# A hybrid transformer layer with 32 experts on one core: expert weights in 2 MB loads with 16 KB rows, other places for them, and side work moved from GpSimd to VectorE

## The chip, the core and the metric

The kernel runs on one core of a Trainium2 chip. TensorE (PE in the profile) multiplies, VectorE (DVE) and ScalarE (ACT) do the elementwise work, GpSimd (POOL) some more of it, and SyncE (SP) issues nearly all DMAs from one queue, in the order in which they are written. Sixteen DMA engines bring the weights from HBM into SBUF. The metric is the device time of one execution in microseconds; less is better. A difference of 0.3% is about what a measurement of this kernel can tell from no change.

## The reference, cut to what matters

One layer over 256 latent tokens that also read 256 context tokens, width 1024, all in float32:

```python
u, uc = modulate(rmsnorm(x, g1), sh1, sc1), modulate(rmsnorm(ctx, g1), sh1c, sc1c)
p = split_proj(u, w_in)               # q k v of an mLSTM, q k v of a differential attention, gates
a = mlstm(p)                          # 4 heads, both directions
b = diff_attention(p, rope)           # 8 heads, rotary embedding on the latent tokens' q and k
y = (sigmoid(p[8]) * (a @ w_a) + sigmoid(p[9]) * (b @ w_b)) @ w_o
x = x + g1 * y
x = x + g2 * moe_ffn(modulate(rmsnorm(x), sh2, sc2))   # router, top 4 of 32 experts
out = rmsnorm(x, final_g)
# an expert: h = t @ w1 + b1  (1024 -> 2048);  act = min(h1,7)*sigmoid(1.702*h1)*(clip(h2)+1);  act @ w2 + b2
```

Each expert has 8 MB of w1 and 4 MB of w2 (in units of 1048576 bytes, as all MB of loads in this document), and all 32 are read in full: 384 MB.

## The kernel before

**Two halves.** The first part (the "front", to about 500 us) does everything up to the router; the rest is a loop over 16 pairs of experts. Both are written out in one program whose order is fixed in the code for each engine.

**The front.** A list of chunks, each a product of the tokens with 512 columns of a weight, runs in steps of 128 rows (`Chunk.step`, 12 matmuls: L572 to L574 and L582 to L584). Every float32 weight is split two steps ahead (`LOOK`) into two float32r halves: ACT casts `wh` (L558), DVE subtracts to get `wl` (L559). After each step `work.tick()` advances generators that do the side work by one `yield` each: `attention` runs `mlstm_unit` (eight units, one started every five ticks: row broadcast L391, exponentials, `Dm` times scores L410, products L420) and then `diff_unit`; `rope_work` turns k and q (`dk`, `dq`) with two shuffles and one product on DVE (L670, L672) and two operations on POOL (L671, L673); `late_b` adds the two gated branches on POOL (L759), casts the sum to `yh` on ACT (L760) and subtracts on DVE (L761); then `scaled_columns` multiplies half of `w_out` by its gate row, on POOL (L829). `ada_rest` (L303) is more DVE work of this kind. `need(...)` in a chunk's `before` or `mid` runs the generators until those named are done.

**The expert loop.** For each expert `expert` adds XG @ w1 to a bias already in PSUM (`bias_of`, L801; w1 at L1044), evaluates the activation on DVE and ACT (L1049 to L1053), does work for other pairs (`between`: bias of the outputs once, scatter L1080, gather L1018, transposes), transposes the activation (L1057) and multiplies by w2 (L1066). PSUM has four `acc` banks; an expert's hidden layer takes two.

**The places.** An expert's weights come as twelve loads of 1 MB, 8 KB in each of 128 partitions: `epiece` takes load n into place `ORDER[n % 18]`. Four places are the front's weight ring (`w`, number 0 in `ORDER`), fourteen (`v1_` to `v14_`) are laid over the front's other buffers after these are closed. A load is issued when the last reader of what lay in its place is done, and SP issues in order: a load that waits holds up all loads written behind it. In the trace the tiles of places are called `v__` and a number, or `w`.

The functions that the change touches, and what calls them:

## Time and profile before

| | |
|---|---|
| median of 3 runs | 1454.1 us (1451.03 to 1454.37) |
| the profiled execution | 1450.5 us, of it the span from first to last instruction 1448.9 us |
| PE, DVE, ACT, POOL busy | 93%, 37%, 19%, 6% of the span |
| front | 0 to about 500 us |
| expert loop | 500 to about 1434 us |
| DMA in the expert loop | 421 GB/s from 550 to 1400 us |

The page cuts the span into 40 slices of 36.2 us. PE's busy share is no measure of how near it is to its peak, because matmuls overlap and their ends are modelled; what matters is which wait ends last in each stretch.

### The profile page before, as it was taken

How to read it: one execution, taken by the hardware profiler on the slowest of the kernel's cores; microseconds unless marked ns; L12 is line 12 of the kernel's file. 1: busy time of each engine (PE TensorE's matmuls, PEld its weight loads, DVE VectorE, ACT ScalarE, POOL GpSimd, SP SyncE). 2: the span in 40 equal slices, each digit the busy share in tenths (PEclk: the TensorE clock that was granted, in tenths of full speed). 3: DMA queues.
4: the chain of work that ended last, by engine and by line, in shares of the span. 5: the costliest groups of instructions: out<-in, count | busy, mean ns of one | idle time of the engine just before them, and what ended most of it. 6: DMA issues, size and time to landing. Idle time of an engine off the chain costs nothing. (4 is left out here: it accounts for less than half of the span.)

```text
span 1448.9 us, 17248 instructions
## 1 busy us (share of the span) xinstructions
PE 1342.2 (93%) x6981; PEld 713.8 (49%) x6981; DVE 538.2 (37%) x1012; ACT 274.4 (19%) x569; POOL 91.7 (6%) x89
## 2 busy tenths in 40 slices
PE   5999899999998999999999999999999999999995
PEld 4778777778997633333333433333333333333331
DVE  3586765776677622221221221221212212122113
ACT  3423335435644300000000000000000000000001
POOL 0030111120024100000000000000000000000000
PEclk9999999999999989999999999999999999999998
DMA  8575353123379599999999999999999999999993
GB/s 354 212 266 191 133 182 116 59 88 117 128 279 399 214 362 421 420 421 420 422 421 420 421 421 420 421 421 420 421 421 421 420 421 421 421 422 420 421 421 157
DMA packets 68801, 483.90 MB, mean 334 GB/s; under 512 B 8355, under 2 KB 8612, under 8 KB 10604
## 3 DMA queue, kind: packets, MB, share of 16 engines
q1 hardware_dynamic: 67948, 480.36, 81.8%
q0 software_dynamic: 768, 2.38, 0.4%
q8 instruction: 57, 0.93, 0.3%
q14 instruction: 28, 0.23, 0.0%
HBM read 481.64 MB, written 1.06 MB: 333 GB/s over the span
## 5 line engine op out<-in xcount | busy, mean ns | idle before, releaser
L1049 DVE TENSOR_SCALAR eg<-acc 128x512 f32<-128x512 f32 x32 | 22.1, 692 | 450.8 <-PE acc L1044 450.8
L1050 ACT ACTIVATE es<-eg 128x512 f32<-128x512 f32 x32 | 20.2, 630 | 742.8 <-DVE eg L1049 742.8
L1074 DVE TENSOR_TENSOR Y<-py,g2r 64x512 f32<-64x512 f32 x64 | 44.1, 689 | 276.0 <-PE py L1066 275.3
L559 DVE TENSOR_TENSOR wl<-w,wh 128x512 fp32r<-128x512 f32 (+1 forms) x160 | 111.1, 703 | 88.0 <-ACT wh L558 87.3
L1044 PE MATMUL acc<-w,XG 128*64 128x512 f32 x512 | 116.1, 595 | 4.9 <-DMA w<-in_w_dram 4.9
L582 PE MATMUL acc<-uh,wh 128*128 128x256 f32 (+1 forms) x328 | 109.1, 333 | 0.1
L584 PE MATMUL acc<-uh,wl 128*128 128x256 f32 (+1 forms) x328 | 105.0, 320 | 2.9 <-DVE wl L559 2.9
L558 ACT CAST wh<-w 128x512 fp32r<-128x512 f32 (+1 forms) x160 | 93.0, 603 | 61.9 <-PE acc L574 31.3
L583 PE MATMUL acc<-ul,wh 128*128 128x256 f32 (+1 forms) x328 | 104.6, 319 | 0.0
L1044 PEld LDWEIGHTS acc<-w,XG 128*64 128x64 f32 x512 | 35.5, 137 | 82.2 <-issue 65.1
L582 PEld LDWEIGHTS acc<-uh,wh 128*128 128x128 f32 x328 | 62.5, 191 | 12.3 <-ACT wh L558 3.4
L584 PEld LDWEIGHTS acc<-uh,wl 128*128 128x128 f32 x328 | 62.3, 190 | 8.8 <-DVE wl L559 4.1
L572 PE MATMUL acc<-wh,uh 128*128 128x512 f32 x160 | 65.0, 406 | 0.7 <-DVE gi L340 0.7
L583 PEld LDWEIGHTS acc<-ul,wh 128*128 128x128 f32 x328 | 62.4, 190 | 4.4 <-DVE ul L286 0.3
L1018 PEld LDWEIGHTS pga<-P,u 128*128 128x128 f32 x512 | 58.4, 192 | 12.5 <-DVE eg L1049 12.2
L573 PE MATMUL acc<-wl,uh 128*128 128x512 f32 x160 | 63.4, 396 | 0.2 <-DVE wl L559 0.2
L574 PE MATMUL acc<-wh,ul 128*128 128x512 f32 x160 | 63.2, 395 | 0.0
L801 PE MATMUL acc<-b1s,cst 128*64 128x512 f32 x256 | 61.7, 603 | 0.0
L1018 PE MATMUL pga<-P,u 128*128 128x128 f32 x512 | 61.4, 278 | 0.3 <-DVE P L931 0.3
L1080 PE MATMUL acc<-Y,PGT 128*128 128x512 f32 x128 | 59.2, 605 | 0.8 <-DVE Y L1074 0.8
L1027 POOL COPY PG<-PG 128x128 f32<-128x128 f32 x16 | 4.7, 295 | 830.7 <-DVE PG L1025 830.7
L303 DVE SCALAR_TENSOR_TENSOR sums<-w,sil,sums 128x512 f32<-128x512 f32 x56 | 45.6, 829 | 0.0
(920 smaller groups left out, 2047.7 us busy)
## 6 DMA issues: line engine op xcount, KB each, us to landing
w<-in_w_dram SPq DMA_DIRECT2D x86, 1024.0 KB, 19.8
w<-in_w_in_dram SPq DMA_DIRECT2D x30, 1024.0 KB, 5.0
w<-in_ada_w_dram SPq DMA_DIRECT2D x24, 1024.0 KB, 6.1
w<-in_w_a_dram SPq DMA_DIRECT2D x4, 1024.0 KB, 5.0
wo<-in_w_o_dram SPq DMA_DIRECT2D x4, 1024.0 KB, 7.0
w<-in_w_b_dram SPq DMA_DIRECT2D x4, 1024.0 KB, 10.6
wk<-in_w_in_dram SPq DMA_DIRECT2D x2, 1024.0 KB, 13.6
rows<-mrow POOLq DMA_DIRECT2D x3, 512.0 KB, 12.3
```

Of the source, the lines that this page charges most:

```text
L558: act.copy(wh[:, 0:n], raw)
L559: dve.tensor_tensor(out=wl[:, 0:n], in0=raw, in1=lanes(wh[:, 0:n]), op=OP.subtract)
L572: mm(self.ps[j], vh[:, k, s], wh, start=st, stop=False)
L573: mm(self.ps[j], vh[:, k, s], wl, start=False, stop=False)
L574: mm(self.ps[j], vl[:, k, s], wh, start=False, stop=sp)
L582: mm(o, wh[:, c], vh[:, k, t0:t1], start=f, stop=False, skip_group_check=g)
L583: mm(o, wh[:, c], vl[:, k, t0:t1], start=False, stop=False, skip_group_check=g)
L584: mm(o, wl[:, c], vh[:, k, t0:t1], start=False, stop=sp, skip_group_check=g)
L801: mm(G[f // 2][64 * (f % 2):64 * (f % 2) + 64], *bias(f), start=True, stop=False)
L1018: mm(p[:, kk, 0:n * CAP], u2[:, tt, k * 128:k * 128 + 128], P[:, tt].rearrange("p e s -> p (e s)"), start=(tt == 0), stop=(tt == 1))
L1044: mm(G[f // 2][64 * (f % 2):64 * (f % 2) + 64], XG[:, k, sw * CAP:sw * CAP + CAP], w[:, f * 512:f * 512 + 512], start=False, stop=(k == KT ...
L1080: mm(p, PGT[parts[dh], 2 * dh + tt, :], Y2[parts[dh], dh], start=True, stop=True)
```

## The change

- **Loads.** w1 and w2 are laid out on the host so that a load of 2 MB has 16 KB in a row for each partition: w1 in four loads of two 128-row blocks, w2 in two loads. Where two places are neighbours (16 KB in one tile) it is one DMA; elsewhere, and for the whole last expert (`fine`), it is two of 1 MB, with 8 KB of each row.
- **Places.** 21 MB of places: `s` (2 MB, in a pool of its own from the start), `A` and `B` (2 MB each, over the weight ring, which is closed with the front), the numbers with 2 in `PLACES` (2 MB) and those with 1 (1 MB). `ORDER` gives ten loads; load number 10 goes to `EXTRA = (15, 3)`; from number 11 on the ten entries of `ORDER` repeat. Room comes from a smaller area for POOL's own DMAs (`dynamic_dma_scratch_size=1024`), for which one small DMA (`B2T`) is cut in two.
- **Side work.** `rope_work` runs all its products on DVE, in four steps with a `yield` between; `late_b` adds on DVE; `scaled_columns` multiplies on DVE and starts at the `mid` of the first w_b chunk, no longer after `late_b`.
- **mLSTM.** `attention` yields twice before its first unit.
- **Bias.** The biases of experts 0 and 1 are both put in PSUM ahead of the router's end (`G01`); `ppos` moves from an `acc` bank to a `pp` bank for that.

```diff
-R1, R2, LOOK = 4, 14, 2
+R1, LOOK = 4, 2
...
-ORDER = (1, 2, 3, 9, 0, 0, 0, 0, 5, 6, 12, 4, 10, 11, 7, 8, 13, 14)
+PLACES = (("A", 2, 0), ("B", 2, 0), (1, 2, 0), (3, 1, 0), (4, 1, 0), (5, 2, 0), (7, 2, 1), (9, 1, 1), (10, 2, 0), (12, 1, 0),
+          (13, 2, 0), (15, 1, 0))
+ORDER = ("s", 1, (3, 9), "A", "B", 5, (12, 4), 10, 7, 13)
+EXTRA = (15, 3)
...
     def attention():
+        for _ in range(2):
+            yield
         yield from pipe([mlstm_unit(h, d) for h in range(4) for d in range(2)], PER_M)
...
-        for i in range(n):
-            dve.stream_shuffle(t[:, i], x[:, i], SWAP16)
-        pool.tensor_tensor(out=x, in0=x, in1=cb, op=OP.mult)
-        dve.tensor_tensor(out=t, in0=t, in1=sb, op=OP.mult)
-        pool.tensor_tensor(out=x, in0=x, in1=t, op=OP.add)
...
+            for j in range(2):
+                dve.stream_shuffle(t[:, j], h[:, j], SWAP16)
+            yield
+            dve.tensor_tensor(out=h, in0=h, in1=cb, op=OP.mult)
+            yield
+            dve.tensor_tensor(out=t, in0=t, in1=sb, op=OP.mult)
+            yield
+            dve.tensor_tensor(out=h, in0=h, in1=t, op=OP.add)
...
-                pool.tensor_tensor(out=t, in0=t, in1=two(t9[0], k), op=OP.add)
+                dve.tensor_tensor(out=t, in0=t, in1=two(t9[0], k), op=OP.add)
...
-            if c:
-                for i in range(2):
-                    yield from scaled_columns(chunks[-1].ws[i])
...
-            pool.tensor_tensor(out=v[:, k], in0=v[:, k], in1=rows_[0][:, 0, 512:1024], op=OP.mult)
+            dve.tensor_tensor(out=v[:, k], in0=v[:, k], in1=rows_[0][:, 0, 512:1024], op=OP.mult)
...
-    chunks[-4].mid = need("attn", "dp1")
+    def mid_b():
+        need("attn", "dp1")()
+
+        def scaled():
+            for i in range(2):
+                yield from scaled_columns(chunks[-1].ws[i])
+        work.add(scaled())
+    chunks[-4].mid = mid_b
...
-    G0 = bias_of(0)
+    G01 = [bias_of(0), bias_of(1)]
...
-    ppos = acc()
+    ppos = pp()
...
+    def epiece(src, fine=False):
+
+        i = nth[0]
         nth[0] += 1
-        return piece(src, k, n, tile_=slot(i))
...
+        where = EXTRA if i == len(ORDER) else ORDER[(i - (i > len(ORDER))) % len(ORDER)]
+        if isinstance(where, tuple):
+            h = [slot(w) for w in where]
+        else:
+            w = slot(where)
+            h = [w[:, 0:2048], w[:, 2048:4096]]
+            if not fine:
+                nc.sync.dma_start(w, src)
+                return h
+        for n in range(2):
+            nc.sync.dma_start(h[n], src[:, n * 2048:(n + 1) * 2048])
+        return h
...
-    r["w1"] = f(i["exp_w1"]).reshape(E, D, 2 * D)
+    r["w1"] = rows(f(i["exp_w1"]).reshape(E * D, 2 * D), 2).reshape(E, 4, 128, 4 * D)
...
-    r["w2"] = rows(f(i["exp_w2"]).reshape(E * D, D), 2).reshape(E, 4, 128, 2 * D)
+    r["w2"] = rows(f(i["exp_w2"]).reshape(E * D, D), 4).reshape(E, 2, 128, 4 * D)
...
-    nc = _bacc.Bacc("TRN2", target_bir_lowering=False, num_devices=1)
+    nc = _bacc.Bacc("TRN2", target_bir_lowering=False, num_devices=1, dynamic_dma_scratch_size=1024)
```

Three places where the engines' rows stand differently. First SP's queue before, from load number 17 (the last that finds a place for the first time; numbers count from 0, a `v` and a number is the place, and the bracket names what the load waits for: DMA queues' semaphores, and the engines whose work must be done).

```order
L151 DMA v14__4879<-in_w1_dram 128x2048 [waits DMASW7_49,DVE_49,DMAHW6_49,PE_49,Activation_49]
L151 DMA v1__4885<-in_w1_dram 128x2048 [waits DMAHW7_49,PE_49]
L151 DMA v2__4891<-in_w1_dram 128x2048 [waits DMAHW0_49,PE_49]
L151 DMA v3__4941<-in_w2_dram 128x2048 [waits DMAHW1_49,PE_49]
L151 DMA v9__4947<-in_w2_dram 128x2048 [waits DMAHW2_49,PE_49]
L151 DMA w_4953<-in_w2_dram 128x2048 [waits DMAHW3_49,PE_49]
L151 DMA w_4959<-in_w2_dram 128x2048 [waits DMAHW4_49,PE_49]
```

The same stretch of SP's queue in the change, loads number 9 to 16; line numbers are those of the changed file.

```order
L1024 DMA v13__4870<-in_w1_dram 128x4096 [waits DMASW0_49,DMASW7_49,DVE_49,DMAHW0_49,PE_49,Activation_49]
L1027 DMA v15__4924<-in_w2_dram 128x2048 [waits DMASW4_49,DMASW6_49,DVE_49,DMAHW1_49,Activation_49,Pool_49]
L1027 DMA v3__4925<-in_w2_dram 128x2048 [waits DMAHW2_49,PE_49]
L1024 DMA ws_4936<-in_w2_dram 128x4096 [waits DMAHW3_49]
L1024 DMA v1__4955<-in_w1_dram 128x4096 [waits DMAHW4_49]
L1027 DMA v3__4965<-in_w1_dram 128x2048 [waits DMAHW5_49,DMAHW2_49,PE_49]
L1027 DMA v9__4966<-in_w1_dram 128x2048 [waits DMAHW6_49]
L1024 DMA vA__4977<-in_w1_dram 128x4096 [waits DMAHW7_49]
L1024 DMA vB__4987<-in_w1_dram 128x4096 [waits DMAHW0_49]
L1024 DMA v5__5030<-in_w2_dram 128x4096 [waits DMAHW1_49]
```

Load 10 is the pair `v15__4924`, `v3__4925` (the first half of expert 1's w2), load 13 the pair `v3__4965`, `v9__4966` (a quarter of expert 2's w1). Before, each load from place 1 on waits for PE's work on the load 18 numbers earlier. Now `v3__4965` waits for PE's work on the second half of load 10, three numbers earlier, and the loads behind it name no wait for PE of their own any more.

DVE's rows before, in the front where k of the first four heads is turned (`rt`, `dk`: rope; `wl`: weight halves; `sums`: `ada_rest`; `dgm`, `Dm`: an mLSTM unit, head 0 and 1):

```order
L395 TENSOR_TENSOR dgm<-pp,fcst 128x256
L670 STREAM_SHUFFLE rt<-dk 128x256 x2
L672 TENSOR_TENSOR rt<-rt,fcst 128x512
L559 TENSOR_TENSOR wl<-w,wh 128x512
L303 SCALAR_TENSOR_TENSOR sums<-w,sil,sums 128x512
L670 STREAM_SHUFFLE rt<-dk 128x256 x2
L672 TENSOR_TENSOR rt<-rt,fcst 128x512
L559 TENSOR_TENSOR wl<-w,wh 128x512
L410 TENSOR_TENSOR Dm<-Dm,S 128x640
L410 TENSOR_TENSOR Dm<-Dm,S 128x256
L559 TENSOR_TENSOR wl<-w,wh 128x512
```

And now, from the same unit's `dgm`:

```order
L401 TENSOR_TENSOR dgm<-pp,fcst 128x256
L685 TENSOR_TENSOR rt<-rt,fcst 128x512
L565 TENSOR_TENSOR wl<-w,wh 128x512
L309 SCALAR_TENSOR_TENSOR sums<-w,sil,sums 128x512
L687 TENSOR_TENSOR dk<-dk,rt 128x2x256
L565 TENSOR_TENSOR wl<-w,wh 128x512
L309 SCALAR_TENSOR_TENSOR sums<-w,sil,sums 128x512
L416 TENSOR_TENSOR Dm<-Dm,S 128x640
L416 TENSOR_TENSOR Dm<-Dm,S 128x256
L681 STREAM_SHUFFLE rt<-dk 128x256 x2
```

Between the unit's `dgm` and its `Dm` there were four shuffles, two products and two `wl`, beside four operations on POOL; now there are one product, one sum of the rope and two `wl`, no POOL, and on PE four weight steps between the unit's broadcast and its products where there were three.

DVE's rows before at the end of the w_b chunks (`tg`: gated branches, `yl`, `yh`: halves of their sum, `wo`: w_out), the additions and `wo` times `rows` being on POOL:

```order
L753 SCALAR_TENSOR_TENSOR tg<-tg,acc 128x512 x2
L761 TENSOR_TENSOR yl<-tg,yh 128x512
L559 TENSOR_TENSOR wl<-w,wh 128x512
L761 TENSOR_TENSOR yl<-tg,yh 128x512
L559 TENSOR_TENSOR wl<-w,wh 128x512
L559 TENSOR_TENSOR wl<-wo,wh 128x512 x2
L753 SCALAR_TENSOR_TENSOR tg<-tg,acc 128x512 x2
L761 TENSOR_TENSOR yl<-tg,yh 128x512
L559 TENSOR_TENSOR wl<-wo,wh 128x512
L761 TENSOR_TENSOR yl<-tg,yh 128x512
L559 TENSOR_TENSOR wl<-wo,wh 128x512 x7
```

And now:

```order
L762 SCALAR_TENSOR_TENSOR tg<-tg,acc 128x512 x2
L837 TENSOR_TENSOR wo<-wo,rows 128x512
L768 TENSOR_TENSOR tg<-tg 128x512
L770 TENSOR_TENSOR yl<-tg,yh 128x512
L565 TENSOR_TENSOR wl<-w,wh 128x512
L837 TENSOR_TENSOR wo<-wo,rows 128x512
L768 TENSOR_TENSOR tg<-tg 128x512
L770 TENSOR_TENSOR yl<-tg,yh 128x512
L565 TENSOR_TENSOR wl<-w,wh 128x512
L837 TENSOR_TENSOR wo<-wo,rows 128x512
L565 TENSOR_TENSOR wl<-wo,wh 128x512
L837 TENSOR_TENSOR wo<-wo,rows 128x512
```

The additions (`tg<-tg`) and the products of `wo` and `rows` now stand between the `wl` rows.

## Rows read from the trace of the kernel before

**Rows 1.** The page's second part: the span in 40 slices of 36.2 us; busy share of PE, share of the DMA engines' time (tenths), and GB/s.

```profile
PE   5999899999998999999999999999999999999995
...
DMA  8575353123379599999999999999999999999993
GB/s 354 212 266 191 133 182 116 59 88 117 128 279 399 214 362 421 420 421 420 422 421 420 421 421 420 421 421 420 421 421 421 420 421 421 421 422 420 421 421 157
```

**Rows 2.** Busy time of each engine by stretch, in the expert loop (from:to in us, length, then each engine's busy us and count, granted clock, DMA share, GB/s).

```profile
550.00:1400.00 850.00, 800.51 (x3809) 305.98 (x3810) 176.06 (x278) 51.95 (x89) 4.12 (x14) 1.00 1.01 421
1400.00:1420.00 20.00, 17.73 (x80) 5.07 (x76) 2.65 (x4) 0.63 (x1) 0.00 (x0) 1.00 1.01 419
1420.00:1430.00 10.00, 7.49 (x30) 2.68 (x32) 1.49 (x3) 0.59 (x1) 0.00 (x0) 0.83 0.37 155
```

**Rows 3.** DVE's timeline, the first operation after an expert's w1 (start us, busy us, engine, line): two early in the expert loop and two later, each time two experts apart.

```profile
547.31 0.69 DVE L1049 TENSOR_SCALAR eg<-acc 128x512 f32<-128x512 f32 x1 [13.20 <-PE acc L1044]
...
603.50 0.69 DVE L1049 TENSOR_SCALAR eg<-acc 128x512 f32<-128x512 f32 x1 [13.20 <-PE acc L1044]
...
999.57 0.69 DVE L1049 TENSOR_SCALAR eg<-acc 128x512 f32<-128x512 f32 x1 [15.94 <-PE acc L1044]
...
1059.20 0.69 DVE L1049 TENSOR_SCALAR eg<-acc 128x512 f32<-128x512 f32 x1 [15.69 <-PE acc L1044]
```

**Rows 4.** PE's timeline at expert 1's w2 and the next bias, and at the last pieces of the last expert's w1 (in brackets the idle time before and what ended it).

```profile
556.20 1.89 PE L1066 MATMUL py<-v__4947,eaT 128*64 128x512 f32 x8
557.92 3.60 PE L1066 MATMUL py<-w,eaT 128*64 128x512 f32 x16
...
1412.47 1.94 PE L1044 MATMUL acc<-v__8446,XG 128*64 128x512 f32 x8 [0.56 <-DMA v__8446<-in_w_dram]
1414.94 1.94 PE L1044 MATMUL acc<-v__8452,XG 128*64 128x512 f32 x8 [0.53 <-SPq L1151]
1417.43 1.94 PE L1044 MATMUL acc<-v__8458,XG 128*64 128x512 f32 x8 [0.56 <-SPq L1151]
```

**Rows 5.** Stretches with shorter rows: from 404.5 us on mostly the broadcasts `rows` and `g2r` (4 KB rows), around 417.7 us mostly `b1` (2 KB rows); then a stretch of 8 KB rows alone. Columns as in rows 2.

```profile
404.50:407.00 2.50, 2.50 (x23) 2.50 (x23) 0.71 (x2) 2.10 (x6) 0.25 (x1) 1.00 1.01 410
...
417.55:417.95 0.40, 0.40 (x6) 0.40 (x4) 0.00 (x0) 0.40 (x3) 0.40 (x1) 1.00 0.94 369
...
510.00:520.00 10.00, 9.48 (x34) 3.38 (x30) 5.89 (x9) 0.88 (x2) 0.00 (x0) 0.91 1.02 428
```

**Rows 6.** The page's third part, a queue that fetches instructions (packets, MB, share of 16 engines' span); and from its sixth a load issued when the DMA engines had little left to do (KB, us from issue to landing).

```profile
q8 instruction: 57, 0.93, 0.3%
...
v__4986<-in_w_dram SPq DMA_DIRECT2D x1, 1024.0 KB, 4.8
```

**Rows 7.** The front at 164 to 177 us: PE, DVE and POOL timelines, and one stretch (columns as in rows 2).

```profile
170.85 3.78 PE L420 MATMUL pp<-mv,Dm 128*128 128x258 f32 x8 [4.17 <-DVE Dm L410]
...
168.22 1.75 DVE L559 TENSOR_TENSOR wl<-w,wh 128x512 fp32r<-128x512 f32 x1
169.90 1.14 DVE L410 TENSOR_TENSOR Dm<-Dm,S 128x640 f32<-128x640 f32 x2
170.96 0.70 DVE L559 TENSOR_TENSOR wl<-w,wh 128x512 fp32r<-128x512 f32 x1
...
167.72 1.70 POOL L671 TENSOR_TENSOR dk<-dk,fcst 128x512 f32<-128x512 f32 x1 [1.40 <-DVE rt L670]
...
170.85:177.00 6.15, 6.15 (x21) 5.39 (x22) 3.75 (x9) 0.51 (x2) 0.25 (x1) 0.51 0.52 181
```

**Rows 8.** Timelines: DVE and one wait of PE at the second rope; DVE, POOL and PE at the last w_b step and w_out (L582 to L584 are w_b, L572 to L574 w_out; matmuls of a step follow each other).

```profile
290.33 1.75 DVE L559 TENSOR_TENSOR wl<-w,wh 128x512 fp32r<-128x512 f32 x1
...
292.13 0.39 PE L584 MATMUL acc<-uh,wl 128*128 128x256 f32 x1 [1.69 <-DVE wl L559]
...
448.30 1.28 DVE L753 SCALAR_TENSOR_TENSOR tg<-tg,acc 128x512 f32<-128x512 f32 x2
...
462.59 10.85 DVE L559 TENSOR_TENSOR wl<-wo,wh 128x512 fp32r<-128x512 f32 x7
...
458.70 13.59 POOL L829 TENSOR_TENSOR wo<-wo,rows 128x512 f32<-128x512 f32 x8
...
452.81 0.39 PE L584 MATMUL acc<-bh,wl 128*128 128x256 f32 x1 [0.73 <-DVE wl L559]
453.03 0.28 PE L582 MATMUL acc<-bh,wh 128*128 128x256 f32 x1
...
455.52 0.39 PE L572 MATMUL acc<-wh,yh 128*128 128x512 f32 x1
...
456.91 0.40 PE L572 MATMUL acc<-wh,yh 128*128 128x512 f32 x1
...
461.02 0.50 PE L573 MATMUL acc<-wl,yh 128*128 128x512 f32 x1 [1.80 <-DVE wl L559]
...
464.39 0.51 PE L573 MATMUL acc<-wl,yh 128*128 128x512 f32 x1 [1.71 <-DVE wl L559]
...
475.56 0.40 PE L572 MATMUL acc<-wh,yh 128*128 128x512 f32 x1
```

**Rows 9.** PE's timeline at the router.

```profile
491.73 3.20 PE L801 MATMUL acc<-b1s,cst 128*64 128x512 f32 x8
495.50 0.19 PE L954 MATMUL acc<-sel,trib 128*128 128x32 bf16 x1 [0.57 <-DVE sel L950]
```

More of the change, by code (lines that the diff above doesn't have):

```diff
@@ L152, in piece @@
         return w[:, 0:k * n].rearrange("p (k n) -> p k n", k=k)
-    fr = ExitStack()
-    early = ctx.enter_context(tc.tile_pool(name="early", bufs=1))
     four = fr.enter_context(tc.tile_pool(name="four", bufs=3))
@@ L326, in lam_work @@
         lp = t2([128, 64], "lp")
-        le = sm.tile([128, 2], F32, name="le")
+        le = sm.tile([128, 2], F32, name="le", tag="ssq1")
         for i in range(2):
@@ L783, in load_rows @@
         bcast(rows[:, 3], a["ng2"])
-        nc.gpsimd.dma_start(B2T, bass.AP(tensor=mrow.tensor, offset=mrow.offset + D, ap=[[1, 128], [128, KT]]))
+        for h in range(2):
+            nc.gpsimd.dma_start(B2T[:, 4 * h:4 * h + 4], bass.AP(tensor=mrow.tensor, offset=mrow.offset + D + 512 * h,
+                                                                 ap=[[1, 128], [128, 4]]))
         pool.tensor_scalar(rows[:, 0], rows[:, 0], 0.5, None, op0=OP.mult)
@@ L984, in hybrid_layer @@
     tp = lambda name, bufs, **kw: ctx.enter_context(tc.tile_pool(name=name, bufs=bufs, reuse_waits="tile", **kw))
-    ring2 = [tp("ring2_%d" % i, 1) for i in range(R2)]
+    ring2 = {i: (tp("ring2_%s" % i, 1), n, pad) for i, n, pad in PLACES}
     mo = tp("mo", 1)
@@ L1137, in between @@
                     nxt["PGT"] = transposed(nxt["P"][1], 2)
-            Y = expert(XG, sw, G0 if e == 0 else bias_of(e), w1p, w2p, between)
+            Y = expert(XG, sw, G01[e] if e < 2 else bias_of(e), w1p, w2p, between)
             evac_y(Y2, Y, sw)
```

63 lines of the change are left out of this document (32 added, 31 removed).

## The prediction

> **What bounds the kernel now.** I read the page's slices first, then stretches, then the rows at the seams. From slice 15 on the DMA engines are full: 421 GB/s, with the engines' time taken to 1.01 [rows 1, 2]. PE is at nine tenths there too, so the next view has to say which of the two sets the pace. The activation's first operation comes every 28.1 us early in the loop (two experts from 547.31 to 603.50) and every 29.8 us later (two experts from 999.57 to 1059.20) [rows 3]. 28.1 us is what PE needs for an expert whose weights lie ready. 29.8 us is what the DMA engines need for 12 MB: 12 x 2.485 us a MB. So the loop starts with a stock of loaded weights, eats it up at 1.7 us an expert, and from about 1000 us on PE waits for landings: at the end each MB of w1 comes 2.48 us after the last, and PE sits idle 0.5 us before it [rows 4]. The end of the program is the landing of the last expert's last w1 (1417.4 us) [rows 4], and 31.5 us behind it to the end of the span, 1448.9. The DMA engines are busy without a hole from 550 us to that landing, so a hole in their work after 550 us, or a change in their rate, goes into the time one for one.
>
> In the front PE is the bound, with short waits for DVE. The front matters because SP can load only into places whose front users are done, and because the first expert starts behind it.
>
> **What the change does to the loads.** It is SP's queue that I look at first. Load 13 takes places 3 and 9. Place 3 was given to the second half of load 10 only three loads earlier, so load 13 waits until PE has used that half: the third and fourth of expert 1's eight w2 blocks. In the profile before these are the matmuls from 556.20, done when the next begin at 557.92 [rows 4]. SP issues in order, so every expert load written behind load 13 waits as well; though by the rows of the order the next ones (9, `A`, `B`, 5, 12 and 4, 10, 7, 13: 15 MB) name no wait for PE. What the DMA engines have until then is loads 0 to 12, 26 MB. Before, the count at 550 us is 384.5 MB (32 experts and the final norm's row, 0.5) less what lands later: 421 GB/s x 850 us is 341.3 MB, then 8.0 and 1.5 [rows 2], together 350.8. So 33.7 MB had landed, 8 MB more than the change can have. The stock that carried PE through its first seventeen experts is gone: from load 13 on PE takes each load as it lands.
>
> **What 16 KB rows give.** No row of the trace has a 16 KB weight row, so I bound it. With 16 engines, 8 KB at 421 GB/s is 311.3 ns of an engine; 4 KB at 410 is 159.8 ns; 2 KB at 369 with a share of 0.94 is 83.5 ns [rows 2, 5]. The steps are 76.3 and 151.5, nearly a doubling, with 8 ns left over for each row. One more doubling gives 311.3 + 303 = 614.3 ns, or 426.7 GB/s; I take 427, 2.456 us a MB, against 421 and 2.491. Bounds: nothing at all (421), or the slope without any fixed part, 303 ns for 8 KB, 432.6 GB/s (2.424 us). A short stretch with 8 KB rows reaches 428 [rows 5], which speaks for a little more. Against it the only 16 KB packets in the trace, instruction fetches, take 0.3% x 16 x 1448.9 / 57 = 1.2 us each [rows 6], twice the weights' time for their bytes. They run beside full weight queues and go elsewhere; I leave them out of the sum.
>
> A rule would undo this term. The Trainium skill, "DMA: Bandwidth & Descriptors", section "Where 436 GB/s comes from", says that for HBM to SBUF the HBM side binds at about 358 GB/s, so that fewer descriptors would bring nothing. The 421 GB/s of this trace lie over that figure, so the figure does not hold here; a ceiling that has nothing to do with row length could still be there, and is a rival below, at 421.
>
> **The front, edit by edit.**
> - *Rope on DVE, mLSTM two ticks later.* At 170.85 us PE has waited 4.17 us for `Dm`. DVE was late because each of its operations beside POOL's rope takes 1.75 us where it takes 0.70 alone. After the wait the granted clock is 0.51 for 6.15 us, the lower of its levels, which costs 3.0 us of work [rows 7]. In the changed order DVE has about 6.8 us of rows between `dk` and that unit's `dgm` (0.6 to 0.7 a row; the `dd` rows 0.2), then 5.1 us to `Dm`; PE has 5.5 us (my estimate from its rows there) and then four weight steps of 1.43 (21 matmuls from 453.03 to 455.52, 0.119 us each, twelve a step [rows 8]). So PE waits about 11.9 - 11.2, say 1 us, and the clock stays. Gain 3.2 + 3.0 = 6.2 us. Bounds: 0 (the wait only moves) and 7.2.
> - *The second rope.* The same slow `wl` holds PE for 1.69 us at 292.13 [rows 8]. In the new order the `wl` in question stands ahead of the rope's longer part. Gain 1.7 us, between 0 and 1.9.
> - *Additions and w_out's products on DVE.* POOL multiplied w_out for 13.6 us, and beside it DVE's `wl` took 1.55 us (seven in 10.85); PE waited 1.80 and 1.71 us [rows 8]. A step undisturbed takes 1.39 (455.52 to 456.91); the ten from 455.52 to 475.56 took 20.04, which is 6.1 too much, and 0.73 had gone at 452.81: 6.8 us to be had. But four additions and eight products, 0.60 each, are 7.2 us more for DVE at the place where it has `wl` every 1.4 us, and it waits 0.75 us for ACT's `yh` between each addition and subtraction. Going down the new rows by hand from the first `tg` evacuation at 448.3 [rows 8], the `wl` of the last two w_b steps end 1.3 and 1.7 us after PE needs them, those of w_out's third and fourth step 2.6 and 1.7. That is 7.3 us lost for 6.8 won: +0.5 us. Bounds: -6.8 (all waits gone) and +4 (the clock falls again).
> - *Biases.* The second bias, 1.7 us at full clock, stands ahead of the router's position product, which began 0.57 us after PE could take it (495.50) with the first bias ending at 494.9 [rows 9]: about 1.1 us later. Expert 1 has its bias already: -1.7. Four output biases now share two banks and wait for DVE: +0.7. Together +0.1.
> - *Smaller area for POOL's DMAs, `B2T` in two:* I see no wait for the gate row in the views of before, and take nothing; were that cover gone, one more small transfer is under the 4.8 us that a lone MB takes [rows 6].
>
> Sum for the front: -6.2 - 1.7 + 0.5 + 0.1 = -7.3 us. PE lets go of place 3 at 557.9 - 7.3 = 550.6 us.
>
> **The sum.** From there: 2.3 us until the first bytes count (a lone MB lands 4.8 us after issue, 2.5 of it at full rate [rows 6]); then 384.5 - 26 - 4 = 354.5 MB to the last w1 at 2.456, 870.6 us; then 3.7 us, since the last engine lags the bytes (before, 348.3 MB had landed from 550 to 1417.4 us by the stretches, where 346.8 were needed: 1.5 MB). Last w1: 550.6 + 2.3 + 870.6 + 3.7 = 1427.2. The tail is written as before, with loads of 1 MB in the last expert: 31.5. Span 1458.7, that is +9.8 us; the profiled execution's 1450.5 becomes 1460.3. Its time lies 3.6 us under the median of the runs, so a median may be up to 1464; I say 1461.
>
> 2 MB loads themselves cost nothing in between: PE works 3.4 us on each while the next takes 4.9 to land, and its 28.1 us an expert stay under the DMA engines' 29.5.
>
> **Rivals.**
> 1. *The rate does not move* (the loads are merely larger). For it: DMA share 1.01 at 421 [rows 2]. Then 354.5 x 2.491 = 883.0: 12.4 us more, about 1473. Chance 0.17.
> 2. *The rate rises over what short rows suggest.* For it: 427 to 428 in short stretches; against: 8 ns a row is all the shorter rows leave. At the 432.6 of the slope the sum falls by 11.3 us to 1449, the same as before. Faster than before by over 0.3% (4.4 us) needs 2.418 us a MB, 433.6 GB/s; at 437 it would be 1440. Chance 0.20, over half of it on the faster side. This is the case of the other sign.
> 3. *w_out's waits go entirely*, the rate as forecast: DVE keeps ahead of PE through the additions. -7.3 us: 1453, no difference. For it: the slow steps lie beside POOL's work; against: the hand count of rows. Chance 0.11.
> 4. *The waits at w_out grow until the clock falls*, or the mLSTM wait only moves: +4 to +7 us, 1466. The 4.17 us wait before one fall speaks for it, the 1.80 and 1.71 us without a fall against it. Chance 0.07.
>
> The forecast itself (a hole of some 30 us in the DMA engines' work, half paid back by the rate) has 0.45, with 1453 to 1468 as its own range. The range over all takes in the bounds of the rate and of the front: 1446 to 1478. Faster by over 0.3%: 0.12 (rival 2). Within 0.3%, about what a measurement can tell: 0.25 (the rest of 2, rival 3, the low end of the forecast). Slower: 0.63.
>
> **What the changed profile would show.** DMA GB/s: one slice or nearly that, between 520 and 550 us, close to empty; then 427 to the end. SP's longest wait in the loop: for PE's w2 matmul, some 30 us, at load 13. The activation's first operation every 29.5 us from the third expert on, none at 28.1. In the front no PE wait over 2 us but the first of all, and no half clock at 170 us; DVE waits of 1 to 3 us at 450 to 466 us. I am wrong if SP passes load 13 before expert 1's w2, if weight bytes come at 421 or at over 433, or if the first expert starts over 12 us earlier.

## The result, and the profile after

The changed kernel takes 1471.7 us (median of 4 runs, 1470.1 to 1472.8) against 1452.6 us of the kernel before (1447.5 to 1454.4): a ratio of 1.0132, with a 95% interval of 1.0118 to 1.0146. It is slower by 19.2 us, where the forecast said 1461, that is +7 over the median shown then. The profiled execution took 1472.8 us, 1471.0 of it span, so it stands 1.1 us over its median; the one of before stood 2.1 under its own.

The page's slices of the changed kernel: PE's busy share, the DMA engines' share (tenths), GB/s.

```profile
PE   5999989999998998998999898989999989889995
...
DMA  8575433223577727999999999999999999999993
GB/s 348 209 257 208 172 122 115 87 86 116 189 301 333 260 88 323 427 424 428 425 426 425 429 424 428 425 427 425 428 426 426 425 427 426 427 425 427 426 422 148
```

Against [rows 1] two things are new: a slice with 88 GB/s, from 515 to 552 us, where there were 362, and 422 to 429 GB/s from 588 us on, up to the last slice, where there were 420 to 422. Stretches show the same more sharply (columns as in [rows 2]):

```profile
500.00:520.00 20.00, 18.14 (x73) 6.18 (x70) 5.53 (x8) 2.67 (x4) 0.00 (x0) 0.94 0.83 324
520.00:540.00 20.00, 18.65 (x66) 6.10 (x67) 4.91 (x9) 1.17 (x2) 0.29 (x1) 0.72 0.12 50
540.00:560.00 20.00, 18.54 (x104) 8.76 (x102) 3.37 (x5) 2.29 (x4) 0.00 (x0) 1.00 0.02 4
560.00:580.00 20.00, 17.12 (x80) 5.42 (x78) 1.38 (x2) 0.00 (x0) 0.00 (x0) 1.00 1.00 413
...
600.00:1400.00 800.00, 737.73 (x3518) 283.02 (x3516) 161.34 (x254) 47.86 (x82) 3.85 (x13) 1.00 1.01 426
```

PE is busy in the hole: it eats the 26 MB that it has. SP's longest wait in 490 to 600 us (what waited for what: us in total, times, longest):

```profile
SPq L1027 <- PE py L1091: 45.0, 1, 45.0
```

And SP's timeline there (start, us, line, what is loaded):

```profile
509.47 0.42 SPq L1024 DMA_DIRECT2D v__4955<-in_w_dram  x1
558.92 0.33 SPq L1027 DMA_DIRECT2D v__4965<-in_w_dram  x1
...
559.77 0.43 SPq L1024 DMA_DIRECT2D vA__4977<-in_w_dram  x1
560.25 0.69 SPq L1024 DMA_DIRECT2D vB__4987<-in_w_dram  x1
```

Load 13 (`v__4965`, place 3) stands from the last issue before it until 558.92: 4.0 us until `v__4925`, the second half of load 10, has landed, then 45.0 us until PE has used it. Loads 14 and 15 leave within 1.4 us of it: they had been ready. PE's timeline gives the ends of the sum, as [rows 4] and [rows 9] did for the kernel before:

```profile
499.77 3.65 PE L1069 MATMUL acc<-ws,XG 128*64 128x512 f32 x16
...
557.00 1.89 PE L1091 MATMUL py<-v__4925,eaT 128*64 128x512 f32 x8
558.71 3.60 PE L1091 MATMUL py<-ws,eaT 128*64 128x512 f32 x16
...
1438.42 1.94 PE L1069 MATMUL acc<-v__8153,XG 128*64 128x512 f32 x8 [0.56 <-DMA v__8153<-in_w_dram]
...
1444.59 5.99 PE L1091 MATMUL py<-v__8180,eaT 128*64 128x512 f32 x16 [0.73 <-ACT eaT L1084]
```

Place 3 was to come free at 550.6 us; it does at 558.7. The last w1 was to be there at 1427.2; it is at 1438.4. The tail was to take 31.5 us; it takes 32.6, with w2's first half at the clock's lower level. So the span came out 12.3 us over the sum: 8.1 from the front and the first two experts, 3.1 from there to the last w1, 1.1 in the tail.

PE makes 1944 step matmuls in each kernel's front. Counting them on PE's timeline gives the front piece by piece (us):

| PE begins | before | after | difference | gained or lost in this piece | forecast for it |
|---|---|---|---|---|---|
| 1st step matmul | 23.0 | 25.6 | +2.5 | +2.5 | 0 |
| 865th (mLSTM and first rope done) | 276.0 | 276.3 | +0.3 | -2.3 | -6.2 |
| 961st (second rope) | 298.4 | 295.7 | -2.7 | -2.9 | -1.7 |
| 1921st (w_a, w_b, w_out) | 478.4 | 475.2 | -3.2 | -0.5 | +0.5 |
| first expert (router, biases) | 500.3 | 499.8 | -0.5 | +2.7 | +1.1 |
| the w2 behind place 3 | 557.9 | 558.7 | +0.8 | +1.3 | -1.0 |

### The profile page after: what moved, and what is told of

It is laid out like the page before. It is cut to its first block, busy times and chain, and to the rows that moved or that the text cites. A ratio compares the mean times of both kernels' runs of the same rounds, so it can differ in the third digit from the quotient of the medians.

```text
span 1471.0 us, 16915 instructions
## 1 busy us (share of the span) xinstructions
PE 1345.8 (91%) x6981; PEld 715.8 (49%) x6981; DVE 536.5 (36%) x1040; ACT 273.6 (19%) x569; POOL 47.4 (3%) x62
## 5 line engine op out<-in xcount | busy, mean ns | idle before, releaser
L1069 PE MATMUL acc<-ws,XG 128*64 128x512 f32 x208 | 47.3, 596 | 6.3 <-DMA ws<-in_w_dram 6.1
L309 DVE SCALAR_TENSOR_TENSOR sums<-w,sil,sums 128x512 f32<-128x512 f32 x56 | 42.6, 776 | 0.0
L1105 PEld LDWEIGHTS acc<-Y,PGT 128*128 128x128 f32 x128 | 23.0, 189 | 36.8 <-issue 22.0
L1107 DVE TENSOR_TENSOR x<-x,acc 128x512 f32<-128x512 f32 x64 | 39.9, 681 | 1.0 <-PE acc L1105 1.0
## 6 DMA issues: line engine op xcount, KB each, us to landing
wk<-in_w_in_dram SPq DMA_DIRECT2D x2, 1024.0 KB, 13.6
v__4732<-in_w_dram SPq DMA_DIRECT2D x1, 2048.0 KB, 20.5
```

The source lines that it names most:

```text
L1069: mm(G[f // 2][64 * (f % 2):64 * (f % 2) + 64], XG[:, k, sw * CAP:sw * CAP + CAP], w[:, f * 512:f * 512 + 512], start=False, stop=(k == KT ...
L1105: mm(p, PGT[parts[dh], 2 * dh + tt, :], Y2[parts[dh], dh], start=True, stop=True)
```

## The experiments

### The hole

**Without the extra place.** Load 10 goes to `s`, and so on round 20 MB.

```diff
-        where = EXTRA if i == len(ORDER) else ORDER[(i - (i > len(ORDER))) % len(ORDER)]
+        where = ORDER[i % len(ORDER)]
```

> The changed kernel without the extra place: load 10 goes to `s`, load 11 to place 1 and so on, 20 MB of places, so that load 13 waits for nothing that was loaded three numbers earlier. Theory A (the stop at load 13 is the loss): loads 10 to 13 go out when PE has used loads 0 to 3 (503 to 514 us), the next one when it has used the first half of expert 0's w2 (about 532); a hole of some 8 us at 525 to 533 instead of 40 us at 519 to 560; the last w1 piece lands at 533.9 + (384.5 - 4 - 28) x 2.461 + 3.7 = 1405, span about 1438, against 1449 of the kernel before and 1471 of the changed one. Rival B (2 MB pieces in fewer places hold PE or SP back in the whole loop, and the stop at load 13 only takes from a stock that would be gone anyway): further holes appear in the DMA engines' work and the span stays above 1460.

Measured: 1440.4 us (1439.6 to 1443.5), 0.9924 of before (0.9899 to 0.9950), span of the profiled execution 1441.7. Stretches where the hole was:

```profile
510.00:525.00 15.00, 13.14 (x46) 4.30 (x42) 6.40 (x10) 2.16 (x3) 0.00 (x0) 0.87 1.00 427
525.00:533.00 8.00, 6.65 (x19) 2.67 (x20) 2.66 (x5) 1.17 (x2) 0.29 (x1) 0.50 0.47 201
```

SP's timeline at loads 13 and 14:

```profile
517.67 0.33 SPq L1024 DMA_DIRECT2D vA__4965<-in_w_dram  x1
535.67 0.33 SPq L1024 DMA_DIRECT2D vB__4975<-in_w_dram  x1
```

Load 13 goes out at 517.7, 41 us earlier than in the changed kernel, although the first expert starts 3.9 us later here (503.7). What is left is a hole from 529 to 537 us. Theory A came within 4 us of the span, about what the 3.9 us of the front make. The kernel with one entry less is some 31 us faster than the changed one, and faster than the kernel before.

**With the extra place, and its second half needed last.** All 21 MB stay; only the pair (3, 9) moves from the third to the last place of the repeated order.

```diff
+LATER = ("s", 1, "A", "B", 5, (12, 4), 10, 7, 13, (3, 9))
...
-        where = EXTRA if i == len(ORDER) else ORDER[(i - (i > len(ORDER))) % len(ORDER)]
+        where = ORDER[i] if i < len(ORDER) else EXTRA if i == len(ORDER) else LATER[(i - len(ORDER) - 1) % len(LATER)]
```

> The changed kernel with its extra place for load 10, and all 21 MB of places; only the pair (3, 9) moves from the third to the last place of the repeated order, so that load 13 goes to `A` and load 20 is the one that needs place 3. Theory A (what costs is that a load waits for one that was issued only three numbers earlier): load 13 goes out when PE has used load 3 (about 514 us), load 14 at about 532 us, a hole of some 8 us as in e1_no_extra, span 1438 to 1443. Rival B (the gain of e1_no_extra came from leaving the extra place out, such as from its two loads of 1 MB or the shifted ring): a wait of SP of 30 us or more remains and the span is above 1460.

Measured: 1440.7 us (1439.8 to 1442.9), 0.9922 of before (0.9905 to 0.9938). SP's timeline at loads 13 and 14:

```profile
513.48 0.33 SPq L1025 DMA_DIRECT2D vA__4965<-in_w_dram  x1
530.30 0.33 SPq L1025 DMA_DIRECT2D vB__4975<-in_w_dram  x1
```

Theory A again. The number of places and the loads are those of the changed kernel; the 31 us hang on which load has to wait for which.

### The rate

**Loads of 1 MB with 8 KB of each row** (the layout in HBM as changed, no extra place):

```diff
-            if not fine:
+            if False:
```

> As e1_no_extra, with every load cut into two of 1 MB with 8 KB from each row; the layout in HBM and the places are the same. Theory A (the rate comes from the row's length): 421 GB/s from 550 us on; last w1 at 533.9 + 352.5 x 2.491 + 3.7 = 1416, span about 1448, 10 us over e1_no_extra. Rival B (the layout in HBM, 16 KB in sequence for each partition, is what helps): 426 GB/s and the span of e1_no_extra, about 1438.

**Loads of 2 MB of two 8 KB rows**, which lie apart in HBM (no extra place):

```diff
-                nc.sync.dma_start(w, src)
+                nc.sync.dma_start(w.rearrange("p (j n) -> p j n", j=2), src.rearrange("j p n -> p j n"))
...
-    r["w1"] = rows(f(i["exp_w1"]).reshape(E * D, 2 * D), 2).reshape(E, 4, 128, 4 * D)
+    r["w1"] = f(i["exp_w1"]).reshape(E, 4, 2, 128, 2 * D)
...
```

> As e1_no_extra with loads of 2 MB, but of two 8 KB rows for each partition that lie apart in HBM (the layout of the kernel before). Theory A (the row's length alone): 421 GB/s, span about 1448, as e3_1mb_8k. Rival B (fewer and larger loads on SP's queue raise the rate): 426 GB/s and about 1438.

Measured: 1450.5 us (10 runs, 1448.8 to 1453.7) and 1451.4 (10 runs, 1450.2 to 1453.5); spans 1448.1 and 1448.7, both forecast at 1448. One stretch of each, first with 1 MB loads, then 2 MB of 8 KB rows, then without the extra place and 16 KB rows:

```profile
600.00:1400.00 800.00, 753.68 (x3590) 288.73 (x3588) 167.01 (x263) 49.08 (x84) 3.83 (x13) 1.00 1.01 421
```

```profile
600.00:1400.00 800.00, 751.36 (x3580) 291.38 (x3578) 166.40 (x262) 49.07 (x84) 3.84 (x13) 0.99 1.01 421
```

```profile
600.00:1400.00 800.00, 756.73 (x3630) 293.75 (x3628) 167.73 (x264) 49.05 (x84) 3.81 (x13) 1.00 1.01 426
```

With 8 KB to a row the rate is 421, in loads of 1 or of 2 MB; with 16 KB it is 426. The row's length alone makes the 10 us between 1440.4 and 1450.5 or 1451.4. The Trainium skill, "DMA: Bandwidth & Descriptors", section "Where 436 GB/s comes from", has the HBM side bind at about 358 GB/s for such transfers; all three rates lie above it and still move with the row, so here it does not bind.

### The front's edits

**All of them undone**, the loads as changed: rope, additions and products on POOL, no delay of the mLSTM, one bias.

```diff
-        for _ in range(2):
-            yield
...
-                dve.tensor_tensor(out=t, in0=t, in1=two(t9[0], k), op=OP.add)
+                pool.tensor_tensor(out=t, in0=t, in1=two(t9[0], k), op=OP.add)
...
-    G01 = [bias_of(0), bias_of(1)]
+    G0 = bias_of(0)
...
```

> The changed kernel with all edits of the front's side work undone (rope, additions and products of w_out on POOL, no two steps of delay for the mLSTM, one expert's bias ahead of the router), loads and places as changed. Theory A (the front's edits gave nothing between them, as the first expert's start at 499.8 us against 500.3 says): place 3 comes free within 2 us of 558.9, span 1469 to 1474. Rival B (the edits gave the forecast 7 us, and something else in the changed kernel took it back, such as the 3.4 us at half clock at 22.6 us): the first expert starts 5 us later or more and the span is 1476 to 1480. Rival C (the edits cost time): first expert at 497 or earlier, span 1468 or less.

Measured: 1478.4 us (1475.9 to 1479.0), 1.0180 of before (1.0145 to 1.0216); first expert at 503.5 us, place 3 free at 564.1. The time and the span (1477.0) are those of rival B, but the first expert starts 3.7 us later than in the changed kernel, not 5 or more; theory A and rival C are out. Between the medians the edits are worth 6.7 us to the changed kernel. That this is close to the forecast 7.3 is luck: of the 5.4 us at place 3, 2.9 are the second rope's, 0.3 the mLSTM's and 1.7 those of expert 1's bias; 3.2 lie in a stretch at w_a (34.4 us against 31.2) that the changed kernel's profile gets through undisturbed and four related profiles below do not; against these go 2.1 us at the first step matmul (23.5 us here, 25.6 there) and 0.7 between the second rope and w_a. And place 3 comes free 6.2 us later here than in the kernel before, whose front has the same side work. The next runs look for what costs that.

**Rope on POOL, mLSTM two steps later** (on the kernel without the extra place, as all that follow unless said otherwise).

```diff
-            dve.tensor_tensor(out=h, in0=h, in1=cb, op=OP.mult)
-            yield
-            dve.tensor_tensor(out=t, in0=t, in1=sb, op=OP.mult)
-            yield
-            dve.tensor_tensor(out=h, in0=h, in1=t, op=OP.add)
...
+        pool.tensor_tensor(out=x, in0=x, in1=cb, op=OP.mult)
+        dve.tensor_tensor(out=t, in0=t, in1=sb, op=OP.mult)
+        pool.tensor_tensor(out=x, in0=x, in1=t, op=OP.add)
```

> e1_no_extra with the rope as before (two operations of four on POOL, all in one step), the mLSTM still two steps later. In e1_no_extra PE waits for `Dm` 1.70, 1.32, 1.53, 0.64 and 1.76 us in 160 to 216 us, 7.0 us together. Theory A (the rope's steps on DVE, one in each of the following steps, delay every later unit's `Dm`): the later waits are gone but for 0.9 us, the first is 4.2 - 2.9 = 1.3 us, and the stretch from PE's 480th to its 864th step matmul takes 117 us in place of 122.2; the wait for `wl` at the second rope (1.7 us) is back. Rival B (the later waits come from the two steps of delay, which put each unit beside other DVE work): the waits stay, stretch 121 to 123 us.

**Rope on DVE, mLSTM not delayed.**

```diff
-        for _ in range(2):
-            yield
```

> e1_no_extra without the two steps of delay of the mLSTM, the rope on DVE in four steps. Theory A (as for f1_rope_pool): the first wait for `Dm` grows from 1.7 to 4.6 us and the clock falls behind it (3 us), the later four stay: the stretch from PE's 480th to its 864th step matmul takes 128 us. Rival B: the first wait grows in the same way but the later ones (5.3 us) are gone: 123 us.

Measured: 1449.3 us (8 runs, 1444.6 to 1455.9) and 1441.3 us (1436.1 to 1441.7), against 1440.4 with both edits. PE's waits in 155 to 232 us: first the changed kernel, then rope on POOL with the delay, then rope on DVE without it.

```profile
161.54 1.54 PE L426 MATMUL pp<-mv,Dm 128*128 128x258 f32 x6 [1.69 <-DVE Dm L416]
173.81 1.98 PE L426 MATMUL pp<-mv,Dm 128*128 128x258 f32 x8 [1.10 <-DVE Dm L416]
188.08 1.57 PE L426 MATMUL pp<-mv,Dm 128*128 128x258 f32 x6 [1.53 <-DVE Dm L416]
201.14 3.28 PE L426 MATMUL pp<-mv,Dm 128*128 128x258 f32 x14 [0.64 <-DVE Dm L416]
```

```profile
161.51 1.54 PE L426 MATMUL pp<-mv,Dm 128*128 128x258 f32 x6 [1.71 <-DVE Dm L416]
168.16 0.69 PE L397 MATMUL pp<-gN,cst 64*128 64x256 f32 x2 [2.00 <-ACT hm L434]
...
200.35 1.22 PE L397 MATMUL pp<-gN,cst 64*128 64x256 f32 x2 [3.42 <-ACT hm L434]
```

```profile
169.33 1.98 PE L426 MATMUL pp<-mv,Dm 128*128 128x258 f32 x8 [1.27 <-DVE Dm L416]
...
183.99 1.54 PE L426 MATMUL pp<-mv,Dm 128*128 128x258 f32 x6 [1.36 <-DVE Dm L416]
208.54 1.54 PE L426 MATMUL pp<-mv,Dm 128*128 128x258 f32 x6 [0.89 <-DVE Dm L416]
```

Both theories missed sizes. From PE's 481st to its 865th step matmul it takes 132.5 us with the rope on POOL and the delay (A said 117, B 121 to 123), and 119.8 with the rope on DVE and no delay (A 128, B 123), against 122.3 with both edits. With all of the front's edits undone (the run above, whose other differences lie behind this stretch) it is 122.8. From the first step matmul to the 865th:

| us | mLSTM not delayed | two steps later |
|---|---|---|
| rope on POOL | 251.0 | 261.0 |
| rope on DVE | 248.0 | 250.7 |

So it is the delay that brings most of the later waits, as B had it, and it costs 2.7 us with the rope on DVE and 10.0 with the rope on POOL, where PE waits for `hm` as well and the granted clock is at 0.50 three times (3.4, 6.8 and 3.4 us long, at 169.5, 200.2 and 224.1 us). The rope on DVE alone gains 3.0 us, and the first wait, which both theories let grow to 4.6 us, is 1.27 us without any delay. Together the two edits gain 0.3, no more than the profiles with both edits differ among themselves (250.4 to 250.8). In the time the 2.7 us do not show by themselves (1441.3 against 1440.4): PE waits 1.80 and 2.94 us at 414 and 422 us in that execution, which is the next matter.

**POOL's small area.** In the kernel without the extra place, the timelines of POOL, of DVE and of PE at its longest wait:

```profile
415.44 0.76 POOL L791 DMA_DIRECT2D B2T<-mrow  x1 [11.56 <-issue]
416.23 2.81 POOL L793 TENSOR_SCALAR rows<-rows 128x1024 f32<-128x1024 f32 x1
418.98 2.97 POOL L794 TENSOR_SCALAR rows<-rows 128x1024 f32<-128x1024 f32 x1
422.04 2.37 POOL L795 TENSOR_TENSOR rows<-rows 128x1024 f32<-128x1024 f32 x1
...
414.99 2.85 DVE L565 TENSOR_TENSOR wl<-w,wh 128x512 fp32r<-128x512 f32 x2 [2.02 <-PE pp L508]
...
421.41 0.39 PE L590 MATMUL acc<-ah,wl 128*128 128x256 f32 x1 [1.83 <-DVE wl L565]
```

The stretch behind that wait:

```profile
422.10:425.50 3.40, 3.04 (x15) 2.75 (x14) 3.00 (x3) 1.99 (x4) 2.31 (x1) 0.50 0.00 0
```

POOL stands 7.5 and 11.6 us at the two halves of `B2T`, and its three operations on `rows` run in one block to 424.4 us, beside DVE's softmax and `wl`; in the kernel before they started one by one as their data came, at 406.8, 413.0 and 416.8 us. Two `wl` take 2.85 us there, where two take 1.29 alone (402.6 us in the kernel before). PE waits 1.83 us and the clock is at its lower level for 3.4. The Trainium skill, "SBUF — State Buffer", section "SBUF: two separate sides", has POOL and a DVE operation with two inputs in SBUF exclude each other at a port pair that they share; the longer `wl` agree with that.

Two runs put it to the test. **`B2T` behind the three operations:**

```diff
-        for h in range(2):
-            nc.gpsimd.dma_start(B2T[:, 4 * h:4 * h + 4], ...)
         pool.tensor_scalar(rows[:, 0], rows[:, 0], 0.5, None, op0=OP.mult)
         pool.tensor_scalar(rows[:, 2], rows[:, 2], 1.0, None, op0=OP.add)
         pool.tensor_tensor(out=rows[:, 2], in0=rows[:, 2], in1=rows[:, 3], op=OP.mult)
+        for h in range(2):
+            nc.gpsimd.dma_start(B2T[:, 4 * h:4 * h + 4], ...)
```

> e1_no_extra with the two small DMAs of `B2T` issued behind POOL's three operations on `rows`, no longer ahead of them. Theory A (POOL stands at the second of these DMAs until 415.4 us, and its three operations, which before ran at 406.8, 413.0 and 416.8 us as their data came, now run in one block at 416.2 to 424.4 us beside DVE's `wl` and softmax, which makes PE wait 1.8 us and more and lets the clock fall to its lower level at 420 to 422 us): the three operations start at about 404, 410 and 414 us; the waits of PE for `wl` in 415 to 426 us stay under 1.0 us; from the first step on `ah` to the first on `bh` PE takes 23 us or so as the kernel before, no half clock there; the first expert starts 3 to 4 us earlier than in e1_no_extra (503.7 us), span 1437 to 1439. Rival B (the waits at w_a are those of the kernel before, only varying from run to run): first expert within 1 us of 503.7 or of 499.6, without order, and the span 1441 to 1443.

**The kernel before with the small area and `B2T` in two** (and the layout of a table in a branch that is not taken):

```diff
-    nc = _bacc.Bacc("TRN2", target_bir_lowering=False, num_devices=1)
+    nc = _bacc.Bacc("TRN2", target_bir_lowering=False, num_devices=1, dynamic_dma_scratch_size=1024)
...
-        nc.gpsimd.dma_start(B2T, ...)
+        for h in range(2):
+            nc.gpsimd.dma_start(B2T[:, 4 * h:4 * h + 4], ...)
...
```

> The kernel before with one part of the change alone: the smaller area for POOL's DMAs, `B2T` in two (and the layout of a table of the branch that is not taken, which the smaller area asks for). Theory A (this part, forecast at nothing, makes POOL stand some 11 us and sends its three operations on `rows` beside DVE's work in one block): the operations start at about 419 us in place of 406.8, PE's waits for `wl` in 415 to 430 us grow from 1.0 us to 3 us or more, and the first expert starts 3 to 5 us later than 500.3; time 1455 to 1458. Rival B: no change, 1452.5. If the 256-column matmuls, one every 0.116 us in the profile before and every 0.113 us in all profiles of the changed kernel and its variants, come at 0.113 us here, the smaller area (with the addresses that it moves) is the cause of that, and 3 us of gain in the front come off these numbers.

Measured: 1437.5 us (1437.1 to 1442.0) for the first, 2.9 under the kernel it is made from; 1456.5 us (10 runs, 1451.8 to 1460.5) for the second, 1.0029 of before (1.0014 to 1.0044). POOL's timeline in the first, then the timelines of POOL and PE in the second, then the stretch behind PE's wait there:

```profile
403.19 2.78 POOL L790 TENSOR_SCALAR rows<-rows 128x1024 f32<-128x1024 f32 x1 [7.29 <-DMA rows<-mrow]
410.99 2.78 POOL L791 TENSOR_SCALAR rows<-rows 128x1024 f32<-128x1024 f32 x1 [5.02 <-DMA rows<-mrow]
414.81 2.36 POOL L792 TENSOR_TENSOR rows<-rows 128x1024 f32<-128x1024 f32 x1 [1.04 <-DMA rows<-in_ng_dram]
```

```profile
417.32 2.82 POOL L787 TENSOR_SCALAR rows<-rows 128x1024 f32<-128x1024 f32 x1
...
422.52 0.39 PE L584 MATMUL acc<-ah,wl 128*128 128x256 f32 x1 [1.81 <-DVE wl L559]
```

```profile
423.20:426.60 3.40, 3.06 (x15) 2.76 (x14) 3.00 (x3) 1.99 (x4) 2.30 (x1) 0.50 0.00 0
```

Theory A has POOL's part right in both, and the second run's time and first expert (504.0 us); PE's part it has wrong in size. In the first run PE still waits 1.31 us (and 0.63 for `wh`) where under 1.0 was expected, the clock is still at 0.50 from 418.6 to 422.0 us, and the first expert starts 1.9 us earlier than in the kernel without the extra place, not 3 to 4: that execution lost 2.0 us at w_out, with the clock at 0.50 from 463.0 to 469.8, and is the slowest of its four (the others took 1437.1 to 1437.9). In the second PE waits 1.81 us in place of 3 or more. From PE's 1537th to its 1729th step matmul it takes 31.5 us in the kernel before, 34.6 in the same kernel with the small area, 33.6 with `B2T` late, and 35.1, 36.6, 36.5 and 36.6 in four other kernels whose front is the changed one (without the extra place, the two of 8 KB rows, the one with the extra place kept). So the small area with `B2T` in two costs time; which of the two makes POOL stand was not tried apart. In the profiled execution of the changed kernel itself it takes 31.2: POOL's block is there too, at 416.2 us, but PE's waits for `wl` are 0.22 and 0.55 us and the clock stays. What the block costs seems to hang on a few tenths of a microsecond between DVE and POOL, which is argued from these waits and not shown, and whether the other runs of the changed kernel paid for it no profile shows.

**Both repairs together**: `B2T` late and no delay of the mLSTM, with no extra place.

> e1_no_extra with the two `B2T` DMAs behind POOL's operations on `rows` (as f5_b2t_late) and without the two steps of delay of the mLSTM (as f2_no_yields). Theory A (the two act in different stretches, at 410 to 426 us and at 150 to 290 us, and each moves the release of the first places and with it the loads): 2.9 us from the first and 2.7 us from the second, 1440.4 - 5.6 = 1434.8 us, between 1433 and 1437. Rival B (a step earlier in the mLSTM changes what lies beside POOL's operations, so that the second gain is lost again at w_a): 1437.5 or more.

**The same with one bias ahead of the router:**

```diff
-    G01 = [bias_of(0), bias_of(1)]
+    G0 = bias_of(0)
...
-    ppos = pp()
+    ppos = acc()
...
```

> g1_best with one bias ahead of the router, as before. Theory A: the router's product and the first expert start 1.1 us earlier; expert 1 pays 1.7 us for its bias, but by then the DMA engines are behind and its loads come no later: 1.1 us less than g1_best. Rival B (the places that PE lets go in expert 1 set the loads): 0.6 us more than g1_best. Within 0.3 us of each other neither is shown.

Measured: 1434.7 us (5 runs, 1434.0 to 1435.0), 0.9876 of before (0.9858 to 0.9895), as theory A had it (1434.8); 1436.9 us (1433.8 to 1438.4) with one bias. The first is faster than both kernels: first expert at 494.3 us, no half clock in the front after 25 us, one wait of PE over 1 us at w_a (1.07 us at 413.8 us). The second is 2.2 us slower between the medians, which neither theory had (1.1 less, 0.6 more), and is not told apart: its runs lie on both sides of the first's, and in its profiled execution the clock is at its lower level from 487.5 to 494.3 us, which the first's is not.

**Only addresses moved**, in the kernel before. What it tests is a difference that the section below takes up: matmuls of 256 columns come closer together with the changed places.

```diff
+    early = ctx.enter_context(tc.tile_pool(name="early", bufs=1))
     ring = ctx.enter_context(tc.tile_pool(name="ring", bufs=R1))
...
-    early = ctx.enter_context(tc.tile_pool(name="early", bufs=1))
```

> The kernel before with the pool `early` opened ahead of the ring, as in the changed kernel; the instructions of PE, DVE, ACT and POOL are the same in the same order, only addresses move. If the addresses of the front's tiles set the distance of 256-column matmuls (0.116 us before, 0.113 us in the changed kernel): 0.113 us here, the front 3 us shorter, the time 1449 to 1450. If not: 0.116 us and 1452.5.

Measured: 1453.4 us (10 runs, 1450.3 to 1455.6), 1.0003 of before (0.9991 to 1.0015), matmuls at 0.116 us as before. The order of the pools is not what brings them closer; nor is POOL's area, since the kernel with that alone has 0.116 too. In both of these kernels, whose instructions at the mLSTM are those of the kernel before, PE waits for `Dm` as long (4.16 and 4.17 us), but the clock is at its lower level for 3.4 us behind it, where the profile before has 6.9.

## Why the prediction was wrong in size

**Right: what happens to the loads.** SP stands at load 13 for place 3, in one wait for PE, as named; it lasted 45.0 us where some 30 stood, since place 3 came free 8.1 us late and SP was there by 514 us. 26 MB had come by then; the activation's first operation comes at 580.3 us for the third expert and at 1439.5 for the last, 29.6 us apart on the mean, where [rows 3] had 28.1 early on. Taking the wait away in two ways gave 31 us.

**Right: the rate.** 427 was forecast and 426 came; 354.5 MB took 879.7 us from the release of place 3, with lead and lag, where the sum had 876.6. Rival 1 (1473 at a rate that stays at 421) has the right time for the wrong reason: at 421 the changed kernel would have been 10 us slower still, by the difference that 8 KB rows make.

**Wrong: the front's -7.3 us**, which came as +0.8. It stood in the sum because the front sets when place 3 comes free. Three steps failed, and the first weighs most.
- *The mLSTM, -6.2, came as -2.3, and most of that is not the edit's.* I followed one unit through DVE's new order and found about 1 us of wait for it; it had 1.69. I did not follow the units behind it, each of which now waits 1.10, 1.53, 0.64, 1.77 and 0.61 us: 7.3 us together, against 4.17 + 0.87 and 3.0 for the fallen clock before, 8.0. The gain is 0.7 us by the waits, 0.3 by the table of the four combinations. The edit that I took for half of the remedy, the delay, is what made the later waits. "The mLSTM wait only moves" was one half of rival 4, at a chance of 0.07. And about half of the 3.0 us for the clock belongs to that one execution: two others of the same instructions had 3.4 us at the lower level there, 1.7 us of work.
- *POOL's smaller area, 0.* I asked who waits for what these DMAs bring and saw nobody. It is POOL that waits to issue them, and three operations stand behind it. Together with `B2T` in two that costs the kernel before 0.29% (0.14 to 0.44), and the kernel without the extra place 2.9 us by the medians. In the profiled execution of the changed kernel it cost nothing, so it is not part of the 8.1 us as the profile has them.
- *The clock at the router and the first expert, 0.* From 482 us to the end of expert 0 it stood at its lower level for 20.5 us, against 13.6 before. The stretches of the changed kernel, then 482 to 550 us in the kernel before and in the changed one:

```profile
22.57:25.98 3.41, 3.41 (x17) 3.41 (x17) 1.90 (x3) 1.30 (x3) 0.00 (x0) 0.50 1.02 423
...
486.80:493.60 6.80, 6.80 (x25) 3.66 (x26) 4.66 (x18) 1.58 (x3) 2.50 (x2) 0.50 0.66 272
517.50:531.20 13.70, 12.35 (x29) 4.30 (x30) 5.86 (x10) 1.17 (x2) 0.29 (x1) 0.50 0.36 153
...
482.00:550.00 68.00, 63.34 (x303) 28.95 (x302) 25.75 (x65) 9.52 (x18) 3.65 (x5) 0.90 0.85 332
482.00:550.00 68.00, 62.62 (x272) 26.56 (x272) 24.15 (x63) 8.93 (x17) 3.65 (x5) 0.85 0.47 180
```

The 6.9 us more are 3.4 us of work, most of the 3.9 us by which the table's last two rows miss (2.7 + 1.3 against 1.1 - 1.0). The bias itself was costed nearly right: with the router at full clock throughout (the kernel with 1 MB loads) 21.9 us pass from the 1921st step matmul to the first expert, and 21.9 in the kernel before with 3.4 us at half clock, which are 1.7 us of work; so it costs some 1.7 us, where 1.1 stood. The first of these rows is most of the 2.5 us at the start; the rest lies just ahead of it, where 64 matmuls (`S<-w,sil`) take 2.99 us in place of 1.96. The other executions show that such stretches come and go with the same orders: of the five profiles of the changed front (with and without the extra place, 8 KB rows twice, extra place kept) two have the one at 22 us, and the one at the router is 6.8, 6.8, 0, 3.4 and 0 us long.

**Right in sign, small:** the second rope gained 2.9 us where 1.7 stood, and w_out came out even (39.2 us from the 1729th step matmul to the 1921st, 39.0 before), where +0.5 stood. That is luck: the hand count had DVE's `wl` late by 2.6 and 1.7 us, but PE's one wait over 1 us there is for ACT, whose `wh` stands behind `yh` and so behind DVE's addition, and the clock falls after it:

```profile
458.67 0.50 PE L578 MATMUL acc<-wh,yh 128*128 128x512 f32 x1 [1.75 <-ACT wh L564]
```

Of the signs that were named, the front's came (no wait of PE over 2 us but the first, no half clock at 170 us), but DVE's waits at 450 to 466 us are of 0.68 to 1.05 us where 1 to 3 stood.

**Not in the sum at all:** matmuls of 256 columns come 0.113 us apart in every kernel that has the changed places, 0.116 in the three that have the old ones, and those of 512 columns 0.231 for 0.234 (medians). From the 1153rd to the 1441st step matmul that is 47.7 us for 48.2; at that pace the 1944 of the front gain some 3.6 us (an estimate), which hid as much of what the front lost. It is the likely reason why the kernel with the front's edits undone gains 2 us on the kernel before up to the 865th (251.0 from the first, against 253.0), which no run showed by itself.

So the forecast's mechanism of the loads carries the result, and its size is off: +19 us in place of +7, because the front, which was to give 7 us of the hole back, was no earlier than before, and 4.2 us came on top behind it. Rows and runs show the mLSTM's part of that. How the rest divides among POOL's area, the clock and the spacing of the matmuls differs from execution to execution, and for the changed kernel's other three it is open.
